# Differential attention: score products alone in one set of PSUM banks, values beside the projections, the output projection cut in steps

## The chip, the core and the metric

The kernel runs on one core of a Trainium2 chip. TensorE (PE) multiplies matrices from SBUF into PSUM, VectorE (DVE) and ScalarE (ACT) do element-wise work and reductions, and queues of transfers (DMA) bring weights from HBM. PSUM has eight banks of 128 x 512 f32; one accumulating product holds one bank. The metric is the time of one execution in microseconds (us), lower is better.

## What is computed

Two networks, one behind the other, on 256 tokens of width 1024. The first has four layers: Fourier mixing, differential attention, latent attention, Fourier mixing, each followed by an MLP of width 4096; the first three layers carry 256 context tokens as well, so their products have 512 columns. The second has two layers of a state-space mixer beside a windowed attention. The change is in layer 1 of the first network, differential attention:

```
def diff_attend(q1, q2, k1, k2, v, lam):
    s1 = einsum("bqhd,bkhd->bhqk", q1, k1) * 64 ** -0.5
    s2 = einsum("bqhd,bkhd->bhqk", q2, k2) * 64 ** -0.5
    p = softmax(s1) - lam * softmax(s2)
    return einsum("bhqk,bkhe->bqhe", p, v)
y = (rms_norm(o, subln_g) * (1 - lam_init)) @ w_o
```

There are eight heads, each with two score matrices and values of width 128. The 256 latent queries see 512 keys, the 256 context queries see the 256 context keys.

## The kernel before

A program written in a tile language: the source gives the work in an order, a scheduler places each instruction on its engine, earlier lines first, later ones ahead of them where the earlier are not ready. A tile is taken from a pool under a tag; `mm` is the tag of four PSUM banks, `aux` that of the other four, `g` that of 41 SBUF tiles.

Products are made in three matmuls of rounded parts (high x high, high x low, low x high; `split` and `loadw` make the parts, a cast on ACT at L396 or L306 and a subtraction on DVE at L397 or L307).

In `diff`, after a start that makes the keys, queries and values of heads 0 and 1, the heads go in four groups of two. A head has three items, `it` 0 and 1 (128 latent queries each, 512 keys) and 2 (the 256 context queries, 256 keys), so a group has six. An item has two steps:

- the scores step, `scores(h, it)`: split the queries (L396, L397), score products into two banks (L1227), row maxima (DVE, L1231, L1233), exponentials (ACT, L1238, into two `g` tiles), their weighted difference (DVE, L1242 to L1247);
- the values step, `values(h, it)`: four transposes of that difference into a bank (L1258), copy to SBUF (ACT, L1260, a `g` tile), four value products, eight matmuls in the trace, into another bank (L1267), copy and squares (ACT, L1269, L1272); after item 2 of a head the root of the mean square and a scaling (DVE, L413 to L421, L1281).

The steps are staggered by one item (`pipe_feed`, lag 1): scores of an item, then "fill" products, then the values step of the item before. Fill of group g is `qkv(g + 1)`: eight tiles, two of keys and two of queries (`kq`, 24 matmuls of 512 columns each, L324 to L327, evacuated by DVE and ACT at L1143 to L1146 and L1183) and four of values (`val`, 24 matmuls of 256 columns, L1199 to L1201, evacuated by ACT at L1202), at 4/3 of a tile to an item. The fill has its banks in `mm`; scores, transposes, values and `finish` have theirs in `aux`.

`finish(h)` transposes a head's output (L1288) and splits it (ACT L1290, DVE L1291, into `g` tiles) for the output projection. It runs in the last group, `DIFF_FIN` says after which items. Fill of the last group is the output projection: `linear_k` holds four output tiles open in all four `mm` banks and adds one head to all four in a step of twelve matmuls (L351 to L353), `DIFF_WO` says how many steps behind which item. The second half of the output projection follows in `tail` (L324 to L327 with 256 columns).

`rows_add(RATES[1])` at each scores step paces unrelated work: units of modulation rows for later layers, each a 1 MB transfer and two or four DVE reductions (L588).

Of the kernel before, what the change touches and what calls it, by code (L numbers as in the profile page):

```python
# [17 lines left out]
P = 128  # L18
# [208 lines left out]
}  # L227
NDT = 5
AHEAD = 200
RATES = (0.35, 0.13, 0.6, 0.0, 0.3)  # L230
START = 12
LEAD = 2
DIFF_WO = (0, 1, 1, 1, 1, 0, 3)
DIFF_FIN = ((0, 1), (2, 3), (4,), (5,), (6,), ())
ORDER = [2, 5, 8, 11, 0, 1, 3, 4, 6, 7, 9, 10] + list(range(12, 24))
SCHED = ((6, 0), (6, 0), (6, 0), (6, 0), (6, 1), (4, 3), (0, 2), (0, 2))
# [5 lines left out]
class Body:  # L242
# [27 lines left out]
    def mm(self, cols=512):  # L270
        return self.ps.tile([P, 512], F32, tag="mm", name=self.nm("mm"))
# [92 lines left out]
    def pipe_feed(self, items, fill, rate):  # L364
        a, b, lag, q = self.pp
        due = 0.0
        for it in items:
            q.append((it, a(*it)))
            due += rate
            while due >= 1.0:  # L370
                next(fill, 0)
                due -= 1.0
            if len(q) > lag:
                it, r = q.pop(0)
                b(*it, r)

    def pipe_end(self, fill, rate):
        a, b, lag, q = self.pp
# [779 lines left out]
    def diff(self, mod, nxt):  # L1158
        nc = self.nc
        I = self.I  # L1160
# [16 lines left out]
        ks, qs, vs = {}, {}, {}  # L1177
# [9 lines left out]
        def kq(g):  # L1187
            yield from self.linear([I["diff_w"][g]], hs, 512, ev_rope(ks), m0=2 * g)
            yield from self.linear([I["diff_w"][8 + g]], hs, 512, ev_rope(qs), m0=2 * g)

        def val(g):
            w = self.loadw(I["diff_w"][4 + g], 8, 256, by="k")
            for j2 in range(2):
                vs[g, j2] = self.g()[:, :512].rearrange("p (j e) -> p j e", e=256)
            for j in range(4):
                ps = self.mm()
                sl = slice(j * P, j * P + P)
                for k in range(8):
                    nc.tensor.matmul(ps[:, :256], hs[k][0][:, sl], w(0, k, 0, 256), start=k == 0, stop=False)  # L1199
                    nc.tensor.matmul(ps[:, :256], hs[k][0][:, sl], w(1, k, 0, 256), start=False, stop=False)  # L1200
                    nc.tensor.matmul(ps[:, :256], hs[k][1][:, sl], w(0, k, 0, 256), start=False, stop=k == 7)  # L1201
                nc.scalar.copy(vs[g, j // 2][:, j % 2, :], ps[:, :256])  # L1202
                yield
# [8 lines left out]
        def scores(h, it):  # L1212


            self.rows_add(RATES[1])
            nq, k0, nk = (1, 0, 512) if it < 2 else (2, 256, 256)
            if h == 0 and it == 0:
                keys(0)
            q = self.split(qs[h][:, it * P:(it + nq) * P])
            if it == 2 and h < 7:  # L1220
                keys(h + 1)
            s = [self.aux(), self.aux()]
            for c in range(nq):
                for n_, (a, b) in enumerate(((0, 0), (0, 1), (1, 0))):
                    for i in range(2):
                        r = slice(64 * i, 64 * i + 64)
                        nc.tensor.matmul(s[i][:, c * nk:c * nk + nk], q[a][r, c * P:c * P + P],  # L1227
                                         kx[h][b][r, k0:k0 + nk], start=n_ == 0, stop=n_ == 2)
            mx, nm, ac, r = [self.sm(4)[:, :2 * nq] for _ in range(4)]
            for i in range(2):  # L1230
                nc.vector.tensor_reduce(out=mx[:, i * nq:i * nq + nq], in_=s[i].rearrange("p (c k) -> p c k", c=nq),  # L1231
                                        axis=AX.X, op=ALU.max)
            nc.vector.tensor_scalar(out=nm, in0=mx, scalar1=-scale, scalar2=None, op0=ALU.mult)  # L1233
            es = [self.g() for _ in range(2)]
            c0 = 4 * h + it
            for i in (1, 0):
                for c in range(nq):
                    nc.scalar.activation(es[i][:, c * nk:c * nk + nk], s[i][:, c * nk:c * nk + nk], AF.Exp,  # L1238
                                         bias=nm[:, i * nq + c:i * nq + c + 1], scale=scale,
                                         accum_out=ac[:, c:c + 1] if i else dac[:, c0 + c:c0 + c + 1])  # L1240

            nc.vector.reciprocal(r[:, :nq], ac[:, :nq])  # L1242
            nc.vector.scalar_tensor_tensor(out=r[:, :nq], in0=r[:, :nq], scalar=nlam, in1=dac[:, c0:c0 + nq],
                                           op0=ALU.mult, op1=ALU.mult)
            for c in range(nq):
                sl = slice(c * nk, c * nk + nk)
                nc.vector.scalar_tensor_tensor(out=es[0][:, sl], in0=es[1][:, sl], scalar=r[:, c:c + 1],  # L1247
                                               in1=es[0][:, sl], op0=ALU.mult, op1=ALU.add)
            return es[0]

        def values(h, it, p):


            g, e0 = h // 2, (h % 2) * P
            nq = 1 if it < 2 else 2
            ps = self.aux()
            for j in range(4):
                nc.tensor.transpose(ps[:, j * P:j * P + P], p[:, j * P:j * P + P], self.ident)  # L1258
            pt = self.g()[:, :512]
            nc.scalar.copy(pt, ps)  # L1260
            if it == 0:
                of[h] = self.g()[:, :512]
            o = self.aux()
            nj = 4 // nq
            for j in range(4):
                jk = j if it < 2 else 2 + j % 2
                nc.tensor.matmul(o[:, j // nj * P:j // nj * P + P], pt[:, j * P:j * P + P],  # L1267
                                 vs[g, jk // 2][:, jk % 2, e0:e0 + P], start=j % nj == 0, stop=j % nj == nj - 1)
            nc.scalar.copy(of[h][:, it * P:(it + nq) * P], o[:, :nq * P])  # L1269
            sq = self.tp.tile([P, 512], F32, tag="sq", name=self.nm("sq"), bufs=2)  # L1270
            for c in range(nq):
                nc.scalar.activation(sq[:, c * P:c * P + P], o[:, c * P:c * P + P], AF.Square,  # L1272
                                     accum_out=dss[:, 4 * h + it + c:4 * h + it + c + 1])
            if it == 2:
                hc = slice(4 * h, 4 * h + 4)
                ep = self.sm(4)
                nc.vector.scalar_tensor_tensor(out=ep, in0=dac[:, hc], scalar=EPS, in1=dac[:, hc],
                                               op0=ALU.mult, op1=ALU.mult)
                self.rstd_of(dss[:, hc], dr[:, hc], 1.0 / P, ep)
                o3 = of[h].rearrange("p (q e) -> p q e", e=P)  # L1280
                nc.vector.tensor_tensor(out=o3, in0=o3, in1=dr[:, hc].unsqueeze(2).to_broadcast([P, 4, P]), op=ALU.mult)  # L1281

        def finish(h):

            ps = self.aux()
            o = of.pop(h)
            for j in range(4):
                nc.tensor.transpose(ps[:, j * P:j * P + P], o[:, j * P:j * P + P], self.ident)  # L1288
            hi, lo = self.pair(512)
            nc.scalar.activation(hi, ps, AF.Copy, scale=sg)  # L1290
            nc.vector.scalar_tensor_tensor(out=lo, in0=ps, scalar=sg, in1=hi.bitcast(F32), op0=ALU.mult,  # L1291
                                           op1=ALU.subtract)
            os_[h] = (hi, lo)

        def ev_kq0(m, ps):
            ev_rope(ks if m < 2 else qs)(m % 2, ps)

        def qkv(g):
            yield from kq(g)
            yield from val(g)  # L1300

        def out(m, ps, streams=BOTH):
            if m == 0:
                self.rows_to(12)
                nxt()
            self.resid(m, ps, streams, mod, 2)
            self.norm_add(m, streams[0][1], streams[-1][2])
# [1 line left out]
        yield from self.head([I["diff_w"][0], I["diff_w"][8]], ev_kq0)  # L1309
        hs = self.nb.hs  # L1310
        yield from val(0)
        wo = self.linear_k([I["diff_w"][12], I["diff_w"][13]], os_, 512, out)
        for g in range(4):
            items = [(h, it) for h in (2 * g, 2 * g + 1) for it in range(3)]
            fill = qkv(g + 1) if g < 3 else wo
            if g == 0:
                self.pipe_begin(scores, values, 1)
            if g < 3:
                self.pipe_feed(items, fill, 4 / 3)
                self.drain(fill)  # L1320
            else:
                for i, it in enumerate(items):
                    self.pipe_feed([it], wo, DIFF_WO[i])
                    for h in DIFF_FIN[i]:
                        finish(h)
            yield
        self.pipe_end(wo, 0)
        for _ in range(DIFF_WO[6]):
            next(wo)
        finish(7)  # L1330
        self.drain(wo)
        yield from self.tail([I["diff_w"][12 + u] for u in (2, 3)], [os_[h] for h in range(8)], out, 4)
# [905 lines left out]
```

## Time and profile before

| | |
|---|---|
| median of 3 runs | 2953.48 us (2946.76 to 2955.89) |
| the profiled execution, its time | 2948.07 us |
| its span | 2946.3 us |
| PE busy | 2863.0 us (97%) |
| DVE busy | 2153.2 us (73%) |
| ACT busy | 1489.9 us (51%) |
| DMA, mean over the span | 156 GB/s |
| mean granted clock of PE | 0.991 |

Busy times are sums over one profiled execution. A line of the trace gives start and duration in us, engine, source line, output and input tiles with their shapes, the count, and in brackets how long the engine had been idle before it and whose end released it. Matmuls overlap in the record, so the distance between starts is a better measure than the duration. PEclk is the granted clock of PE as a share of full speed.

### The profile page before, as it was taken

The numbers are of one execution on the slowest core, as the hardware profiler recorded it, in microseconds if no ns is written. First come the engines' busy times: TensorE is split into PE (matmuls) and PEld (weight loads), VectorE is DVE, ScalarE is ACT, GpSimd is POOL, SyncE is SP. The second block draws the span as 40 slices with busy tenths as digits, with TensorE's granted clock in tenths as the row PEclk, the third lists the DMA queues.
The fourth block names the chain that finished last, engine by engine and source line by source line (L and its number), as shares of the span: only waits on it lengthen the run. The fifth ranks groups of instructions, "written<-read, shape, count | busy, mean of one in ns | idle before, by whom it ended". The sixth has DMA issues, their size and how long they took to land.

```text
span 2946.3 us, 51090 instructions
## 1 busy us (share of the span) xinstructions
PE 2863.0 (97%) x20316; PEld 2593.5 (88%) x20316; DVE 2153.2 (73%) x4707; ACT 1489.9 (51%) x2941; POOL 18.0 (1%) x66
## 2 busy tenths in 40 slices
PE   8999999998999999999999999999999999999999
PEld 6788889886888888599999999988999999989999
DVE  5597667775986667677756789886666799886765
ACT  5433323554432334855555567655554567655553
POOL 1000000000000000000000000000000000000000
PEclk9999999999999999999999999999999999999999
DMA  9454443320375553145525534333444444333553
GB/s 343 172 200 159 170 160 135 115 87 15 129 284 214 205 196 108 43 169 205 199 99 191 184 138 160 132 115 115 146 172 173 146 156 144 129 116 130 185 186 129
DMA packets 70366, 460.81 MB, mean 156 GB/s; under 512 B 7792, under 2 KB 9840, under 8 KB 16752
## 3 DMA queue, kind: packets, MB, share of 16 engines
q1 hardware_dynamic: 69984, 456.51, 43.6%
q8 instruction: 160, 2.62, 0.4%
q10 hardware_dynamic: 144, 1.05, 0.1%
q14 instruction: 78, 0.64, 0.1%
HBM read 456.47 MB, written 1.05 MB: 155 GB/s over the span
## 4 chain that ended last, share of the span: by engine, by line
PE 85%; DVE 8%; ACT 4%; DMA 1%; issue 1%; ACTq 0%; SPq 0%; DVEq 0%
PE mm L324 23%; PE mm L325 23%; PE mm L327 22%; DVE wlo L307 2%; ACT whi L306 1%; PE mm L675 1%; PE mm L674 1%; PE mm L676 1%; PE aux L1267 1%; PE mm L745 1%; PE aux L545 1%; PE mm L746 1%; PE mm L744 1%; DVE t L1701 1%; PE aux L1227 1%
## 5 line engine op out<-in xcount | busy, mean ns | idle before, releaser
L324 PE MATMUL mm<-g,whi 128*128 128x256 f32 (+3 forms) x5008 | 1406.9, 310 | 12.9 <-DVE t L1701 6.0
L325 PE MATMUL mm<-g,whi 128*128 128x256 f32 (+3 forms) x5008 | 1400.4, 308 | 0.5 <-DVE g L397 0.5
L306 ACT CAST whi<-raw 128x1024 fp32r<-128x1024 f32 (+2 forms) x670 | 697.5, 1048 | 821.0 <-PE mm L325 723.7
L324 PEld LDWEIGHTS mm<-g,whi 128*128 128x128 f32 x5008 | 941.6, 188 | 75.6 <-issue 15.7
L325 PEld LDWEIGHTS mm<-g,whi 128*128 128x128 f32 x5008 | 941.3, 188 | 51.7 <-issue 3.1
L307 DVE TENSOR_TENSOR wlo<-raw,whi 128x1024 fp32r<-128x1024 f32 (+2 forms) x670 | 809.5, 1210 | 122.0 <-ACT whi L306 65.7
L327 PE MATMUL mm<-g,wlo 128*128 128x256 f32 (+3 forms) x5008 | 835.2, 308 | 0.0
L327 PEld LDWEIGHTS mm<-g,wlo 128*128 128x128 f32 x5008 | 712.8, 188 | 47.0 <-issue 0.7
L588 DVE CUSTOM_DVE_ANT_0 junk<-raw,silu_b 128x1024 bf16<-128x1024 f32 x208 | 253.8, 1220 | 46.8 <-DMA raw<-in_mod_wT 44.9
L607 DVE SCALAR_TENSOR_TENSOR x<-mm,mod,x 128x256 f32<-128x256 f32 x216 | 98.3, 479 | 129.1 <-PE mm L327 125.4
L769 DVE TENSOR_TENSOR y<-mm,rb 128x256 f32<-128x256 f32 (+1 forms) x144 | 61.3, 427 | 89.8 <-PE mm L327 68.5
L846 DVE TENSOR_TENSOR g<-t,g 128x256 fp32r<-128x256 f32 (+2 forms) x192 | 98.5, 514 | 4.2
L843 ACT ACTIVATE t<-t 128x256 f32<-128x256 f32 (+2 forms) x192 | 94.0, 491 | 8.0 <-DVE g L846 2.9
L1701 DVE SCALAR_TENSOR_TENSOR t<-mm,cwh,t 128x270 f32<-128x270 f32 (+2 forms) x192 | 91.9, 490 | 2.7 <-ACT t L1698 2.4
L2195 DVE TENSOR_TENSOR x<-x,mm 128x272 f32<-128x272 f32 (+1 forms) x64 | 27.5, 429 | 81.0 <-PE mm L327 81.0
L675 PE MATMUL mm<-g,whi 128*128 128x256 f32 x240 | 66.7, 287 | 1.7 <-DVE g L643 1.6
L676 PE MATMUL mm<-g,wlo 128*128 128x256 f32 x240 | 65.5, 282 | 0.0
L841 ACT ACTIVATE t<-mm 128x512 f32<-128x512 f32 x64 | 37.9, 600 | 53.7 <-PE mm L327 53.6
L845 DVE CAST g<-t 128x256 fp32r<-128x256 f32 (+2 forms) x192 | 64.0, 334 | 1.3 <-ACT t L843 0.9
L674 PE MATMUL mm<-g,whi 128*128 128x256 f32 x240 | 60.7, 285 | 2.6 <-ACT g L642 2.6
L744 PE MATMUL mm<-g,whi 128*128 128x258 f32 (+2 forms) x192 | 54.5, 287 | 1.0 <-ACT g L716 0.7
L745 PE MATMUL mm<-g,whi 128*128 128x258 f32 (+2 forms) x192 | 54.7, 286 | 0.3 <-DVE g L717 0.3
(409 smaller groups left out, 3270.9 us busy)
## 6 DMA issues: line engine op xcount, KB each, us to landing
raw<-in_mlp_w SPq DMA_DIRECT2D x128, 1024.0 KB, 4.9
raw<-in_w_in SPq DMA_DIRECT2D x76, 1024.0 KB, 4.9
raw<-in_mod_wT SPq DMA_DIRECT2D x72, 1024.0 KB, 4.9
raw<-in_w_up SPq DMA_DIRECT2D x32, 1024.0 KB, 4.8
raw<-in_w_dn SPq DMA_DIRECT2D x32, 1024.0 KB, 4.8
raw<-in_diff_w SPq DMA_DIRECT2D x16, 1024.0 KB, 4.8
raw<-in_w_sd SPq DMA_DIRECT2D x16, 1024.0 KB, 4.8
raw<-in_mod_w SPq DMA_DIRECT2D x13, 1024.0 KB, 5.3
```

Of the source, the lines that this page charges most:

```text
L306: nc.scalar.copy(hi, v)
L307: nc.vector.tensor_tensor(out=lo, in0=v, in1=hi.bitcast(F32), op=ALU.subtract)
L324: mm(ps, w(0, k, c0, c1), xs[k][0], start=first and k == 0, stop=False)
L325: mm(ps, w(0, k, c0, c1), xs[k][1], start=False, stop=False)
L327: mm(ps, w(1, k, c0, c1), xs[k][0], start=False, stop=last and k == n - 1)
L588: nc.vector.tensor_tensor_reduce(out=self.junk, in0=r[:, D * j:D * j + D], in1=self.silu_b[:, D * s:D * s + D], scale=1.0, scalar=0.0, op0 ...
L607: self.nc.vector.scalar_tensor_tensor(out=self.x[m][:, c0:c1], in0=ps[:, c0:c1], scalar=mod[:, gc * 8 + m, s:s + 1], in1=self.x[m][:, c0:c ...
L675: mm(pss[i][:, c0:c1], w(0, k, o, o + P), l, start=False, stop=False)
L676: mm(pss[i][:, c0:c1], w(1, k, o, o + P), h, start=False, stop=k == 7)
L843: nc.scalar.activation(s[:, :n], t[:, :n], AF.Square)
L846: nc.vector.tensor_tensor(out=lo, in0=s[:, :n], in1=hi.bitcast(F32), op=ALU.subtract)
L1701: nc.vector.scalar_tensor_tensor(out=t[:, sft:L2], in0=ps[:, :L2 - sft], scalar=cw[:, 3 - sft:4 - sft], in1=t[:, sft:L2], op0=ALU.mult, op ...
```

## The change

- `RATES[1]` goes from 0.13 to 0: no modulation rows are issued from the scores steps of this layer.
- The values step takes its two banks from `mm` instead of `aux`, and so does `finish`, except for the last item (7, 2) and for head 7. `aux` is then left to the score products.
- `linear_k` is replaced for this projection by `wo_gen`, in ten steps: seven that add one of heads 0 to 6 to two output tiles (six matmuls each), two that take heads 0 to 6 into one further tile each (21 matmuls), one that adds head 7 to all four (12 matmuls) and evacuates them.
- `held` traces a fill step so that its PE instructions come behind a given matmul in PE's queue: the last score matmul traced, or, after item (7, 2), its last value matmul.
- `val(3)`, the values of the last two heads, goes from the fill of group 2 to the last group, four steps behind the scores of item (6, 0). Group 2 keeps `kq(3)` at 2/3 of a tile to an item.
- `DIFF_WO` then says, for the six items of the last group: 4 (of `val(3)`), 1, 1, 2, 1, 2 steps; one more before the last values step and one behind it.

```
@@ -227,10 +227,10 @@
 }
 NDT = 5
 AHEAD = 200
-RATES = (0.35, 0.13, 0.6, 0.0, 0.3)
+RATES = (0.35, 0.0, 0.6, 0.0, 0.3)
 START = 12
 LEAD = 2
-DIFF_WO = (0, 1, 1, 1, 1, 0, 3)
+DIFF_WO = (4, 1, 1, 2, 1, 2, 1, 1)
 DIFF_FIN = ((0, 1), (2, 3), (4,), (5,), (6,), ())
 ORDER = [2, 5, 8, 11, 0, 1, 3, 4, 6, 7, 9, 10] + list(range(12, 24))
 SCHED = ((6, 0), (6, 0), (6, 0), (6, 0), (6, 1), (4, 3), (0, 2), (0, 2))
@@ -373,6 +373,14 @@
             if len(q) > lag:
                 it, r = q.pop(0)
                 b(*it, r)
+
+    def held(self, gen):
+
+        while True:
+            with self.tc.issue_after(self.behind.ins):
+                if next(gen, self) is self:
+                    return
+            yield
 
     def pipe_end(self, fill, rate):
         a, b, lag, q = self.pp
@@ -1224,8 +1232,9 @@
                 for n_, (a, b) in enumerate(((0, 0), (0, 1), (1, 0))):
                     for i in range(2):
                         r = slice(64 * i, 64 * i + 64)
-                        nc.tensor.matmul(s[i][:, c * nk:c * nk + nk], q[a][r, c * P:c * P + P],
-                                         kx[h][b][r, k0:k0 + nk], start=n_ == 0, stop=n_ == 2)
+                        self.behind = nc.tensor.matmul(
+                            s[i][:, c * nk:c * nk + nk], q[a][r, c * P:c * P + P], kx[h][b][r, k0:k0 + nk],
+                            start=n_ == 0, stop=n_ == 2)
             mx, nm, ac, r = [self.sm(4)[:, :2 * nq] for _ in range(4)]
             for i in range(2):
                 nc.vector.tensor_reduce(out=mx[:, i * nq:i * nq + nq], in_=s[i].rearrange("p (c k) -> p c k", c=nq),
@@ -1253,19 +1262,24 @@
 
             g, e0 = h // 2, (h % 2) * P
             nq = 1 if it < 2 else 2
-            ps = self.aux()
+
+            bank = self.aux if (h, it) == (7, 2) else self.mm
+            ps = bank()
             for j in range(4):
                 nc.tensor.transpose(ps[:, j * P:j * P + P], p[:, j * P:j * P + P], self.ident)
             pt = self.g()[:, :512]
             nc.scalar.copy(pt, ps)
             if it == 0:
                 of[h] = self.g()[:, :512]
-            o = self.aux()
+            o = bank()
             nj = 4 // nq
             for j in range(4):
                 jk = j if it < 2 else 2 + j % 2
-                nc.tensor.matmul(o[:, j // nj * P:j // nj * P + P], pt[:, j * P:j * P + P],
-                                 vs[g, jk // 2][:, jk % 2, e0:e0 + P], start=j % nj == 0, stop=j % nj == nj - 1)
+                last = nc.tensor.matmul(o[:, j // nj * P:j // nj * P + P], pt[:, j * P:j * P + P],
+                                        vs[g, jk // 2][:, jk % 2, e0:e0 + P], start=j % nj == 0,
+                                        stop=j % nj == nj - 1)
+            if (h, it) == (7, 2):
+                self.behind = last
             nc.scalar.copy(of[h][:, it * P:(it + nq) * P], o[:, :nq * P])
             sq = self.tp.tile([P, 512], F32, tag="sq", name=self.nm("sq"), bufs=2)
             for c in range(nq):
@@ -1282,7 +1296,7 @@
 
         def finish(h):
 
-            ps = self.aux()
+            ps = self.aux() if h == 7 else self.mm()
             o = of.pop(h)
             for j in range(4):
                 nc.tensor.transpose(ps[:, j * P:j * P + P], o[:, j * P:j * P + P], self.ident)
@@ -1292,6 +1306,33 @@
                                            op1=ALU.subtract)
             os_[h] = (hi, lo)
 
+        def wo_gen():
+
+
+            mm = nc.tensor.matmul
+            ws = [self.loadw(I["diff_w"][12 + u], 8, 256) for u in range(2)]
+            pss = {}
+
+            def part(m, ks):
+                if m not in pss:
+                    pss[m] = self.mm()
+                w, c0 = ws[m // 2], m % 2 * P
+                for k in ks:
+                    for a, b in ((0, 0), (0, 1), (1, 0)):
+                        mm(pss[m], w(a, k, c0, c0 + P), os_[k][b], start=k == 0 and a + b == 0, stop=k == 7 and a == 1)
+
+            for k in range(7):
+                part(0, (k,))
+                part(1, (k,))
+                yield
+            for m in (2, 3):
+                part(m, range(7))
+                yield
+            for m in range(4):
+                part(m, (7,))
+                out(m, pss[m])
+            yield
+
         def ev_kq0(m, ps):
             ev_rope(ks if m < 2 else qs)(m % 2, ps)
 
@@ -1309,24 +1350,27 @@
         yield from self.head([I["diff_w"][0], I["diff_w"][8]], ev_kq0)
         hs = self.nb.hs
         yield from val(0)
-        wo = self.linear_k([I["diff_w"][12], I["diff_w"][13]], os_, 512, out)
+        wo = wo_gen()
         for g in range(4):
             items = [(h, it) for h in (2 * g, 2 * g + 1) for it in range(3)]
-            fill = qkv(g + 1) if g < 3 else wo
+            fill = kq(3) if g == 2 else qkv(g + 1) if g < 2 else val(3)
             if g == 0:
                 self.pipe_begin(scores, values, 1)
             if g < 3:
-                self.pipe_feed(items, fill, 4 / 3)
+                self.pipe_feed(items, fill, 4 / 3 if g < 2 else 2 / 3)
                 self.drain(fill)
             else:
                 for i, it in enumerate(items):
-                    self.pipe_feed([it], wo, DIFF_WO[i])
+                    self.pipe_feed([it], self.held(wo if i else fill), DIFF_WO[i])
                     for h in DIFF_FIN[i]:
                         finish(h)
             yield
+        held = self.held(wo)
+        for _ in range(DIFF_WO[6]):
+            next(held)
         self.pipe_end(wo, 0)
-        for _ in range(DIFF_WO[6]):
-            next(wo)
+        for _ in range(DIFF_WO[7]):
+            next(held)
         finish(7)
         self.drain(wo)
         yield from self.tail([I["diff_w"][12 + u] for u in (2, 3)], [os_[h] for h in range(8)], out, 4)
```

## Rows read from the trace of the kernel before

**Rows 1.** Windows: stretch, length, busy us of PE, PEld, DVE, ACT, POOL, PEclk, DMA.

```profile
533.60:633.40 99.80, 98.88 (x626) 82.73 (x625) 76.81 (x202) 54.04 (x157) 0.00 (x0) 1.00 0.28 98
633.40:680.60 47.20, 46.71 (x302) 39.23 (x301) 33.20 (x97) 26.27 (x82) 0.00 (x0) 1.00 0.17 61
680.60:745.50 64.90, 49.82 (x261) 37.22 (x261) 34.14 (x98) 28.60 (x89) 0.00 (x0) 0.89 0.05 17
```

**Rows 2.** Timeline of PE, scores and values steps around items (7, 0) and (7, 1).

```profile
709.24 1.06 PE L1227 MATMUL aux<-g,g 64*128 64x512 f32 x6
710.22 0.66 PE L1258 MATMUL aux<-k,g 128*128 128x128 f32 x4
...
713.88 1.16 PE L1267 MATMUL aux<-g,g 128*128 128x128 f32 x8 [0.44 <-ACT g L1260]
714.88 0.60 PE L1288 MATMUL aux<-k,g 128*128 128x128 f32 x4
...
717.27 0.98 PE L1227 MATMUL aux<-g,g 64*128 64x512 f32 x6
...
722.57 1.16 PE L1267 MATMUL aux<-g,g 128*128 128x128 f32 x8 [1.43 <-ACT g L1260]
```

**Rows 3.** Timeline of ACT in the same stretch.

```profile
711.90 0.69 ACT L1238 ACTIVATE g<-aux,sm 128x512 f32<-128x512 f32 x1 [2.96 <-DVE sm L1233]
...
713.25 0.58 ACT L1260 COPY g<-aux 128x512 f32<-128x512 f32 x1
...
716.43 0.32 ACT L396 CAST g<-g 128x128 fp32r<-128x128 f32 x1
```

**Rows 4.** Timeline of PE behind the scores of item (6, 0).

```profile
681.53 0.66 PE L1258 MATMUL aux<-k,g 128*128 128x128 f32 x4
686.68 2.08 PE L1267 MATMUL aux<-g,g 128*128 128x128 f32 x8 [4.49 <-ACT g L1260]
688.54 1.91 PE L1288 MATMUL aux<-k,g 128*128 128x128 f32 x8
```

**Rows 5.** Timeline of PE behind item (7, 2), last values to second half.

```profile
733.51 1.16 PE L1267 MATMUL aux<-g,g 128*128 128x128 f32 x8 [0.67 <-ACT g L1260]
738.64 1.09 PE L1288 MATMUL aux<-k,g 128*128 128x128 f32 x4 [3.97 <-DVE g L1281]
740.51 2.08 PE L351 MATMUL mm<-g,whi 128*128 128x512 f32 x4 [0.78 <-ACT g L1290]
...
745.54 0.28 PE L324 MATMUL mm<-g,whi 128*128 128x256 f32 x1
```

**Rows 6.** Timeline of PE: a tile of keys, a tile of values.

```profile
534.52 0.50 PE L324 MATMUL mm<-g,whi 128*128 128x512 f32 x1
...
540.18 0.40 PE L324 MATMUL mm<-g,whi 128*128 128x512 f32 x1
...
562.89 0.28 PE L1199 MATMUL mm<-whi,g 128*128 128x256 f32 x1
...
565.72 0.60 PE L1258 MATMUL aux<-k,g 128*128 128x128 f32 x4
```

**Rows 7.** Timeline of PE behind a tile of keys, transposes of (1, 2).

```profile
588.46 0.60 PE L1258 MATMUL aux<-k,g 128*128 128x128 f32 x4
588.81 0.47 PE L324 MATMUL mm<-g,whi 128*128 128x512 f32 x1
```

**Rows 8.** Timeline of ACT in the same stretch.

```profile
589.56 0.37 ACT L1183 COPY g<-mm 128x256 f32<-128x256 f32 x1 [0.37 <-DVE t L1144]
589.83 0.59 ACT L1260 COPY g<-aux 128x512 f32<-128x512 f32 x1
```

**Rows 9.** Timeline of PE, windowed attention of the second network.

```profile
2004.69 0.65 PE L2001 MATMUL mm<-ptm,vz 128*64 128x256 f32 x2 [0.20 <-DVE ptm L1992]
```

**Rows 10.** Groups by line from 533.6 to 745.5, modulation rows on DVE.

```profile
L588 DVE CUSTOM_DVE_ANT_0 junk<-raw,silu_b 128x1024 bf16<-128x1024 f32 x8 | 9.7, 1218 | 1.6 <-DMA raw<-in_mod_wT 1.6
```

**Rows 11.** Windows, MLP of layer 1, columns as in rows 1.

```profile
800.00:820.00 20.00, 20.00 (x88) 16.25 (x87) 19.97 (x37) 9.68 (x15) 0.00 (x0) 1.00 0.71 259
```

## Prediction, before the change was run

> **What bounds the kernel now.** The page comes first: PE is busy for 97% of the span, so only stretches in which PE waits can give anything. The windows by stage show where layer 1's attention has them: from the first scores step to the start of group 2 PE idles 99.80 - 98.88 = 0.92 us, in group 2 0.49 us, in group 3 up to the second half of the output projection 64.90 - 49.82 = 15.08 us, with the granted clock at 0.89 [rows 1]. PE's timeline names the waits: 4.49 us behind the scores of (6, 0), 3.97 us ahead of the last `finish`, and 0.4 to 1.5 us ahead of the value products of each item [rows 2, 4, 5]. The two long ones halve the clock behind them: eight value matmuls take 2.08 us against 1.16, eight `finish` transposes 1.91 against some 0.95 (two of the fours that take 0.60 each, overlapping), and the last twelve matmuls of the open tiles 745.54 - 740.51 = 5.03 us against 12/24 of 5.66 = 2.83 [rows 2, 4 to 6]. With the last `finish` (1.09 against 0.60) the slow clock costs 0.9 + 1.0 + 0.5 + 2.2 = 4.6 us. All that the change can win in this layer is 15.08 + 0.92 + 0.49 + 4.6 = 21.1 us.
>
> **What sets these waits.** The reader is to follow item (7, 0). Its scores start at 709.24, the transposes of (6, 2) end at 710.9, ACT is idle for 2.96 us until 711.90, and yet the copy of those transposes starts only at 713.25, behind the exponentials of (7, 0) [rows 2, 3]. Both write `g` tiles, the exponentials first in the source. The queries of (7, 1) are cast at 716.43, behind that copy and behind a `finish`, though they had been there for long [rows 3]. The same in PSUM: for 4.49 us PE did nothing although the transposes of heads 0 and 1 were ready and one of the four `aux` banks was free; they came right behind the value products, whose tile stands ahead of theirs in the source [rows 4]. I read this as: tiles of one tag get their buffers in source order, whether buffers are free or not. Then the loop of an item is closed through `g`: scores, maxima, exponentials, copy of the transposes, value products, `finish`, cast of the next queries, scores. From scores to value products it takes 4.64 and 5.30 us, mean 4.97 [rows 2]; without the scores (0.98) and the transposes (0.35, [rows 7]) PE has 3.6 us to fill. From the end of the value products to the next scores it takes 717.27 - 714.88 = 2.39 us, without `finish` (0.35) 2.0 us. Before, fill tiles in `mm` have nothing to do with `aux` and run in all these holes.
>
> **Scores alone in `aux`: worth nothing.** The next scores wait for the cast of their queries, which stands behind the copy in `g`, not for a bank. The Trainium skill (Perfetto Trace Analysis, Identifying Performance Opportunities) says that the same gap coming again and again on the engine that should be full can mean that there isn't enough SBUF or PSUM for the next tile. By it the four banks would take the waits away; that is the first rival below, and the free bank of [rows 4] speaks against it.
>
> **Values beside the fill in `mm`: the cost.** Now the tile of the next fill stands behind the two tiles of a values step in the same tag. Between the transposes of an item and its value products PE can open nothing. Before it does just that: at 588.81 it starts the next tile [rows 7]. The windowed attention of the second network has this order already (its output and the fill in `mm`), and waits for the copy with fill to spare [rows 9]. The price per values step of groups 0 to 2 is:
>
> - Behind a tile of keys or queries. The tile (5.66 us, [rows 6]) covers the 3.6 us; then come the transposes, to 588.81, and the copy can start only when ACT has evacuated the tile: 589.83, plus 0.59 = 590.42 [rows 7, 8]. Wait 1.6 us.
> - Behind a tile of values (2.83 us, [rows 6]): 3.6 - 2.83 = 0.8 us.
> - Behind both: only transposes, copy, values, 0.67 us as at 733.51 [rows 5].
> - Behind no tile: 3.6 us.
>
> Groups 0 and 1 at 4/3 give 1, 1, 1, 2, 1, 1 tiles and one at the end; the eleven values steps stand behind keys or queries 5 times, behind both 2 times, behind values 4 times: 5 x 1.6 + 2 x 0.67 + 4 x 0.8 = 12.5 us, before 0.92: +11.6. Group 2 at 2/3 gives 0, 1, 0, 1, 1, 0 (the sum of the thirds stays a rounding under 1) and one at the end: 3 x 1.6 + 3 x 3.6 = 15.6, before 0.49: +15.1. Bounds: if the copy came ahead of the tile's evacuation, the 1.6 would be 0.67 (8 x 0.93 = 7.4 us less); if next fill opened all the same, nothing is added (second rival).
>
> **Group 3, with `val(3)`, `wo_gen` and `held`.** PE's work is the same matmuls. `val(3)` fills the 4.49 us behind (6, 0) and the 21 matmuls of the second single-tile step, held behind the last value product (21/24 x 5.66 = 4.95 us) fill the 3.97 us ahead of the last `finish`, so the clock does not fall there: these gains are real. But the loop of the five items between does not get shorter, and it is filled with less: a step is now 6/24 x 5.66 = 1.4 us instead of 2.8, and being held behind the scores it no longer runs ahead of them. From scores to values: three items with one step wait 3.6 - 1.4 = 2.2, two with two steps 0.8: 8.2 us. From values to the next scores 5 x 2.0 = 10.0 us, with no open work allowed in. At the ends: copy behind `val(3)` 0.67, copy behind the first 21 matmuls 0.67, `finish` to head 7's matmuls 0.78 [rows 5]: 2.1 us. Together 20.3 us against 15.08 + 4.6 = 19.7 before: +0.6.
>
> **The clock.** PE waits of 3.97 and 4.49 us were followed by a halved clock, those of 0.4 to 1.5 us were not [rows 2, 4, 5]. The three of 3.6 us in group 2 lie nearest to 3.97; I charge each 0.9 + 1.0 = 1.9 us, 5.6 in all (bounds 0, and 9.4 more if the five of 2.0 to 2.2 us do the same).
>
> **Modulation rows.** `RATES[1] = 0` takes a few units out of this layer; eight reductions of 1.218 us are seen in it [rows 10]. DVE is not what PE waits for here, so it gives nothing. They are done in the MLP behind, where the paced count stays and three more units have four reductions instead of two: 6 x 1.22 = 7.3 us of DVE. DVE is full there in places (19.97 of 20.00 us) while PE waits for nothing (20.00 of 20.00) [rows 11]; PE's own matmuls hide it. I take 0, the bound is +7.3. No DMA is late: the three 1 MB transfers only move.
>
> **Sum.** 11.6 + 15.1 + 0.6 + 5.6 = 32.9 us, on the profiled execution's 2948.07 (span 2946.3 and 1.8 around it): 2981.0 us. Its time is 5.4 us under the median of the three runs, inside their scatter of 9; I leave the sum on it.
>
> **The rivals.**
>
> - *The banks were the limit* (faster, 2930 us). If the next scores do run ahead into the wait for the copy, PE has the next item's work in each hole, and what is left is the 2.1 us at the ends: 2948.1 - 21.1 + 2.1 = 2929 to 2930. For it: four banks for two items' scores, and all 15 us of waits stand ahead of tiles in `aux`. Against it: the cast at 716.43 behind the copy [rows 3], and the free bank [rows 4]. It decides where the new waits of the stage stay under 19 us in sum.
> - *The order in `mm` doesn't bind* (no change, 2949 us). Fill opens across a values step as before; groups 0 to 2 keep their 1.4 us, group 3 gives +0.6. For it: nothing shows the order in `mm` in this layer before. Against it: [rows 4, 9].
> - *More of the same* (slower, 2990 to 2998 us): the waits of 2 us halve the clock too (+9.4), or the moved rows make the MLP's weights late (+7.3). For it: DVE's 19.97 of 20. Against it: 1.43 us waits at full clock.
>
> **Numbers.** Chances: the forecast 0.63, more of the same 0.10, no change 0.11, faster 0.16. The forecast's own range is 2968 (copy ahead of the evacuation, no slow clock: 32.9 - 7.4 - 5.6 = 19.9) to 2998. The range for all reaches down to 2940, past the case of no change, and up to 2998; it leaves out most of the faster case. This kernel can be told from no change by 0.3%, about 9 us; the cases give faster 0.16, same 0.11, slower 0.73.
>
> **What would show it.** Right: in the trace after, PE idle ahead of L1267 in nearly every item of groups 0 to 2 with ACT's copy as releaser, some 28 us up to the scores of (6, 0), three of over 3 us in group 2 with a slow stretch behind; the scores of an item still behind the value products of the item before the last; no wait of 4 us in group 3, but 2 us ahead of L1227 in each item. Wrong: scores of two items back to back on PE, or keys and queries tiles that start between L1258 and L1267.

## The result, and the profile after

The changed kernel takes 2991.31 us (median of 4 runs, 2990.74 to 2998.08), the kernel before 2951.49 us (4 runs): a ratio of 1.0138, interval 1.0122 to 1.0153. The forecast was 2981.0, in a range of 2940 to 2998, slower at 0.73. The profiled execution is the longest of the four (span 2996.3 us, 50.0 over that of before), so the stretches below are compared with each other, not with the medians. Of the 50.0 us, 45.9 lie in the stage that the change touches; what lies behind it takes 5.5 us more, what lies ahead of it 1.4 less.

The windows by stage of the changed kernel, from the first scores to the scores of (4, 0), to those of (6, 0), and to the second half of the projection; they answer to [rows 1]:

```profile
core 0: us, PE busy (x) PEld busy (x) DVE busy (x) ACT busy (x) POOL busy (x), PEclk, DMA share, GB/s
532.20:647.50 115.30, 101.64 (x613) 84.13 (x612) 68.22 (x184) 54.09 (x158) 0.00 (x0) 0.97 0.16 55
647.50:712.12 64.62, 45.51 (x217) 35.09 (x216) 33.79 (x96) 25.92 (x78) 0.00 (x0) 0.87 0.15 49
712.12:789.96 77.84, 64.55 (x357) 51.24 (x357) 34.79 (x99) 29.57 (x88) 0.00 (x0) 0.89 0.04 14
```

The reader is to see length less PE busy: PE idles 13.66, 19.11 and 13.29 us, 46.06 in all, where it idled 0.92, 0.49 and 15.08 before. The stage is 257.76 us long, 45.86 more than before; idle time is 29.6 of that. Most of the rest is the clock (0.97, 0.87 and 0.89 granted). These are the stretches at half clock in the stage:

```profile
core 0: us, PE busy (x) PEld busy (x) DVE busy (x) ACT busy (x) POOL busy (x), PEclk, DMA share, GB/s
584.07:587.49 3.42, 3.42 (x18) 3.42 (x17) 0.00 (x0) 1.55 (x4) 0.00 (x0) 0.50 0.00 0
642.10:645.51 3.41, 3.41 (x16) 3.41 (x17) 0.48 (x2) 0.59 (x4) 0.00 (x0) 0.50 0.00 0
652.34:659.17 6.83, 6.08 (x20) 4.63 (x21) 3.97 (x17) 2.10 (x10) 0.00 (x0) 0.50 0.06 24
...
sum 40.96, PE 38.59 PEld 31.85 DVE 13.76 ACT 14.02 POOL 0.00; mean PE 4.29 PEld 3.54 DVE 1.53 ACT 1.56 POOL 0.00
```

PE works 38.6 us at half speed. At full speed this would take about half as long (eight value products take 1.16 us in place of 2.08), so I put the cost at 19.3 us, an estimate that e10 tests below: 3.4 in groups 0 and 1, 7.6 in group 2, 8.3 in group 3. The two stretches of before (683.79 to 690.62, 738.41 to 745.23) cost 4.9 by the same reading.

PE's waits in the stage, by what ended them (L1278 are the value products, L1271 the copy of the transposes, L1235 the scores, L404 and L405 the split of the queries):

```profile
engine line waited for: us in total, times, longest us
PE mm L1278 <- ACT g L1271: 37.6, 22, 4.1
PE aux L1235 <- ACT g L404: 4.0, 4, 1.5
PE aux L1235 <- DVE g L405: 1.2, 3, 0.6
```

Before, value products waited 9.7 us in 8 places. PE's timeline at three places (L1269 transposes; in brackets the idle time ahead of an instruction and what ended it):

```profile
545.41 0.60 PE L1269 MATMUL mm<-k,g 128*128 128x128 f32 x4
547.40 1.16 PE L1278 MATMUL mm<-g,g 128*128 128x128 f32 x8 [1.39 <-ACT g L1271]
548.32 0.48 PE L324 MATMUL mm<-g,whi 128*128 128x512 f32 x1
...
648.39 0.66 PE L1269 MATMUL mm<-k,g 128*128 128x128 f32 x4
653.09 2.08 PE L1278 MATMUL mm<-g,g 128*128 128x128 f32 x8 [4.04 <-ACT g L1271]
655.10 1.65 PE L1235 MATMUL aux<-g,g 64*128 64x512 f32 x6
...
732.36 0.73 PE L1235 MATMUL aux<-g,g 64*128 64x512 f32 x4 [1.46 <-ACT g L404]
```

At 545.41 transposes, 1.39 us of nothing, values, and only then the next keys tile (L324), where before that tile started behind the transposes [rows 7]. At 648.39 the same with no fill ahead of it: 4.04 us, and the values behind it take 2.08 us in place of 1.16. At 732.36 scores that wait for the cast of their queries, though all of `aux` is theirs.

### The profile page after: what moved, and what is told of

Same layout as the page of the kernel before. It is cut to its first block, busy times and chain, and to the rows that moved or that the text cites. A ratio compares the mean times of both kernels' runs of the same rounds, so it can differ in the third digit from the quotient of the medians.

```text
span 2996.3 us, 51094 instructions
## 1 busy us (share of the span) xinstructions
PE 2883.2 (96%) x20316; PEld 2607.2 (87%) x20316; DVE 2154.9 (72%) x4707; ACT 1490.8 (50%) x2941; POOL 18.0 (1%) x66
## 4 chain that ended last, share of the span: by engine, by line
PE 83%; DVE 9%; ACT 5%; DMA 1%; issue 1%; ACTq 0%; DVEq 0%; SPq 0%
PE mm L324 23%; PE mm L325 22%; PE mm L327 22%; DVE wlo L307 3%; PE mm L1278 1%; PE mm L683 1%; ACT whi L306 1%; PE mm L682 1%; PE mm L684 1%; ACT g L1247 1%; PE aux L1235 1%; PE mm L753 1%; PE mm L754 1%; PE mm L752 1%; DMA raw<-in_mlp_w 1%
## 5 line engine op out<-in xcount | busy, mean ns | idle before, releaser
L324 PE MATMUL mm<-g,whi 128*128 128x256 f32 (+3 forms) x5008 | 1411.2, 311 | 14.7 <-DVE t L1745 6.0
L324 PEld LDWEIGHTS mm<-g,whi 128*128 128x128 f32 x5008 | 945.5, 189 | 80.0 <-issue 16.3
L683 PE MATMUL mm<-g,whi 128*128 128x256 f32 x240 | 66.7, 286 | 1.7 <-DVE g L651 1.6
L1278 PE MATMUL mm<-g,g 128*128 128x128 f32 x184 | 30.5, 316 | 37.6 <-ACT g L1271 37.6
L1247 ACT ACTIVATE g<-aux,sm 128x512 f32<-128x512 f32 (+1 forms) x64 | 36.5, 578 | 57.9 <-DVE sm L1242 47.2
L1278 PEld LDWEIGHTS mm<-g,g 128*128 128x128 f32 x184 | 25.8, 216 | 43.6 <-ACT g L1271 43.5
```

The lines of the kernel that those rows point to most:

```text
L324: mm(ps, w(0, k, c0, c1), xs[k][0], start=first and k == 0, stop=False)
L683: mm(pss[i][:, c0:c1], w(0, k, o, o + P), l, start=False, stop=False)
```

## The experiments

Eleven kernels. Idle time and slow clock were read for each as above, in one profiled execution of each kernel, between the same four points. The stage is the whole from the first scores to the second half of the projection, "slow clock" the estimated cost of the stretches at half clock, in us by the same groups; "-" is under 0.1. Code is shown in short.

| kernel | median, us | ratio to before, 95% | stage, us | PE idle, groups 0-1 / 2 / 3 | slow clock |
|---|---|---|---|---|---|
| before | 2950.1 to 2951.5 | | 211.9 | 0.9 / 0.5 / 15.1 | - / - / 4.9 |
| changed | 2991.3 | 1.0122 to 1.0153 | 257.8 | 13.7 / 19.1 / 13.3 | 3.4 / 7.6 / 8.3 |
| e1 values in `aux` | 2955.5 | 1.0004 to 1.0029 | 217.0 | 0.9 / 3.6 / 14.5 | - / 0.5 / 6.1 |
| e2 output bank early | 2963.1 | 1.0030 to 1.0068 | 220.7 | 1.0 / 5.5 / 12.8 | - / 1.7 / 6.6 |
| e3 before, values in `mm` | 2974.2 | 1.0056 to 1.0103 | 234.7 | 13.5 / 7.5 / 13.5 | 1.7 / - / 4.9 |
| e4 before, rate 0 | 2953.2 | 0.9992 to 1.0014 | 212.9 | 0.9 / 0.6 / 15.1 | - / - / 5.2 |
| e5 fill back | 2984.5 | 1.0100 to 1.0130 | 238.7 | 13.6 / 7.5 / 17.2 | - / - / 6.1 |
| e10 pads | 2987.3 | 1.0108 to 1.0153 | 248.5 | 1.8 / 4.3 / 13.6 | - / - / 6.7 |
| e6 queries' own tile | 2950.5 | 0.9989 to 1.0010 | 207.1 | 4.8 / 5.3 / 4.4 | - / - / - |
| e9 the same, pairs of banks | 2954.7 | 1.0008 to 1.0032 | 202.6 | 0.3 / - / 6.2 | - / - / 1.7 |
| e7 before, queries' own tile | 2947.3 | 0.9974 to 0.9994 | 205.0 | 1.3 / 0.7 / 9.9 | - / - / 4.5 |
| e11 before, own tile and pairs | 2943.5 | 0.9963 to 0.9985 | 201.6 | 0.8 / 0.2 / 3.9 | - / - / 3.3 |
| e12 changed, own tile and pairs | 2944.1 | 0.9970 to 0.9989 | 204.1 | 0.3 / - / 6.2 | - / - / 3.4 |

**Is it the place of the values?** One part undone (e1), one part alone (e3):

```
e1: - bank = self.aux if (h, it) == (7, 2) else self.mm
    + bank = self.aux if h < 6 or (h, it) == (7, 2) else self.mm
e3 (in before): + bank = self.mm if h < 6 else self.aux     # for ps and o in values
```

> The changed kernel with the values step of heads 0 to 5 back in aux; group 3 and the fill of 2/3 in group 2 as changed. Theory (the values tiles in mm bar the next fill tile): PE's idle time in groups 0 and 1 falls from 13.7 us to about 1 and their 3.4 us of slow clock go; in group 2 the holes can be filled again, but with two thirds of a tile to an item the loop of an item, some 7.4 us, sets the pace: idle from 19.1 to about 8, slow clock from 7.6 to about 2. Sum 12.7 + 3.4 + 11 + 5.6 = 33 us less: about 2958 us. Rival (the thin fill of group 2 and the smaller steps of group 3 are the cost, not the place of the values): groups 0 and 1 gain their 16 us and group 2 nothing: 2975 us.

> The kernel before with one part alone: the values step of heads 0 to 5 in mm. Theory (order in mm): groups 0 and 1 get the 12.7 us of idle time and 3.4 us of slow clock that the changed kernel shows, group 2, still filled at 4/3, half of that again: 2951 + 24 = 2975 us. Rival (the loss comes from the thin fill and the cut projection, and order in mm does not matter): 2951 us.

e1, its windows by stage:

```profile
533.05:631.19 98.14, 97.24 (x614) 81.18 (x613) 66.75 (x183) 52.79 (x156) 0.00 (x0) 1.00 0.19 65
631.19:672.86 41.67, 38.07 (x217) 29.29 (x217) 33.45 (x98) 24.85 (x78) 0.00 (x0) 0.99 0.23 77
672.86:750.03 77.17, 62.68 (x357) 50.64 (x357) 33.62 (x97) 30.22 (x91) 0.00 (x0) 0.92 0.04 14
```

Of the 45.9 us that the stage lost, 257.8 - 217.0 = 40.8 go with the place of the values, the other 5.1 with the thin fill, the cut projection and the rate together; no run tells these three apart in this kernel. Group 2 kept 3.6 us of idle time, not the 8 expected: with `mm` free, two thirds of a tile nearly suffice. e3 shows the same from the other side, 2974.2 against 2975 expected.

**Order or number of banks?** e2 leaves the values in `mm` and the order of the tiles, and only opens the output's bank before the wait:

```
  for j in range(4): nc.tensor.transpose(ps[:, ...], p[:, ...], self.ident)
+ o = bank()
+ if h < 6: nc.tensor.transpose(o[:, :P], p[:, :P], self.ident)   # overwritten by the values
  pt = self.g()[:, :512]; nc.scalar.copy(pt, ps)
```

> The changed kernel, values of heads 0 to 5 still in mm, but each output bank is opened ahead of the copy: one more transpose (128 columns, its result overwritten by the value products) is written into it right behind the transposes. Number of banks and order of tiles stay. Theory (the fill tile waits because the output tile ahead of it in the source has not been opened yet): fill starts in the wait again, and the gain is that of the values in aux, 33 us, less 18 transposes of some 0.1 us: about 2960 us. Rival (four mm banks are too few for values and fill): no gain, 2991 to 2993 us.

PE's timeline of e2 at the place shown above (L1272 is the extra transpose, L1280 the values):

```profile
546.91 0.60 PE L1269 MATMUL mm<-k,g 128*128 128x128 f32 x4
547.35 0.27 PE L1272 MATMUL mm<-k,g 128*128 128x128 f32 x1
547.37 0.48 PE L324 MATMUL mm<-g,whi 128*128 128x512 f32 x1
...
549.56 1.05 PE L1280 MATMUL mm<-g,g 128*128 128x128 f32 x8
```

The next keys tile starts 0.02 us after the extra transpose does, and the 1.39 us are gone: 2963.1 us, 28 less than the changed kernel, with no bank added and 18 instructions more. The wait was one of order. The Trainium skill (Perfetto Trace Analysis, Identifying Performance Opportunities) says that a gap which repeats on the engine that should be full can mean too little SBUF or PSUM for the next tile. Here the gap did come back with every item, and what waited was the next tile in PSUM, but the number of banks was enough: the 1.39 us went with the same four, one of them taken earlier.

**Does the cost depend on the fill ahead of the wait?** e5 makes `val(3)` in group 2 again, at 4/3:

```
- fill = kq(3) if g == 2 else qkv(g + 1) if g < 2 else val(3)
+ fill = qkv(g + 1) if g < 3 else iter(())          # rate 4/3 in all three, DIFF_WO[0] = 0
```

> The changed kernel with one part undone: the values of heads 6 and 7 are made in group 2 again, whose fill is 4/3 of a tile to an item as before; values in mm, cut projection and held steps stay. Theory (a values step in mm waits the shorter, the more fill lies ahead of it): group 2 pays what half of groups 0 and 1 pay, 6.8 us of idle time and 1.7 of slow clock in place of 19.1 and 7.6, 18 us less; the wait behind the scores of (6, 0) comes back with its slow clock, some 6 us: about 2979 us. Rival (a values step in mm costs the same whatever the fill): only the 6 us, 2997 us.

Group 2 of e5:

```profile
644.25:701.82 57.57, 50.09 (x314) 41.31 (x313) 35.20 (x99) 27.77 (x82) 0.00 (x0) 1.00 0.16 56
```

It does: group 2 idles 7.5 in place of 19.1 us, and its clock stays full. Group 3 took the wait of [rows 4] back (4.04 us) and idles 17.2. The stage is 19.1 us shorter than in the changed kernel, the median only 6.8: 2984.5 lies 5.5 over the theory's 2979 and 12.5 under the rival's 2997. In the profile, 6.2 us of the gain are lost again behind the stage, where the instructions are the same; the last section comes back to this.

**What is the clock worth by itself?** e10 keeps the waits of groups 0 to 2 and puts matmuls of no use into them:

```
+ PADS = ((5, 5, 3), (3, 7, 5), (5, 5, 3), (3, 7, 16), (5, 16, 5), (5, 16, 5))
  (in values, behind the transposes, h < 6:)
+ with self.tc.issue_after(tlast.ins):
+     for _ in range(PADS[h][it]):
+         nc.tensor.matmul(pad, kp[:, :P], kp[:, :512], start=True, stop=True)
```

> The changed kernel with idle time of PE filled by matmuls of no use: behind the transposes of each values step of heads 0 to 5, 3 to 16 extra matmuls (512 columns, 0.23 us each at full clock) into a bank of aux that nobody reads, about as many as fit the wait seen there. The waits for the copy stay as long, PE is only not idle in them. Theory (half of what the prediction missed is the clock that falls behind waits of 1.8 to 4.1 us): the half-speed stretches of groups 0 to 2 go and with them 3.4 + 7.6 us: about 2980 us. Rival (the slow clock costs nothing by itself, since the matmuls in it would have waited anyway): 2991 us, or some 2 more for matmuls that do not fit the wait.

Its timeline at the place of the 4.04 us (L1275 pads, L1284 values) and its windows of groups 0 to 2:

```profile
645.84 0.66 PE L1270 MATMUL mm<-k,g 128*128 128x128 f32 x4
646.25 3.90 PE L1275 MATMUL aux<-g 128*128 128x512 f32 x16
650.53 1.16 PE L1284 MATMUL mm<-g,g 128*128 128x128 f32 x8 [0.37 <-ACT g L1277]
```

```profile
532.81:644.95 112.14, 110.32 (x665) 89.43 (x665) 68.24 (x184) 54.01 (x158) 0.00 (x0) 1.00 0.17 57
644.95:702.70 57.75, 53.47 (x282) 41.05 (x281) 33.67 (x96) 25.91 (x78) 0.00 (x0) 1.00 0.15 55
```

The wait for the copy is as long (from the start of the transposes to the values 4.69 us, in the changed kernel 4.70), the values take 1.16 us again, and the two stretches are 3.2 and 6.9 us shorter than in the changed kernel, close to the 3.4 and 7.6 read as the price of the clock. In the medians the 11 us expected are only 4, and the intervals of the two ratios overlap: the stretches show the price, the whole time doesn't.

**What holds the scores back?** e6 gives the split of the queries an SBUF tile of its own (and `g` 40 tiles in place of 41); e7 does it in the kernel before:

```
- q = self.split(qs[h][:, it * P:(it + nq) * P])
+ qt = self.mixp.tile([P, 512], F32R, tag="q", bufs=1); q = qt[:, :n], qt[:, n:2 * n]   # n = nq * P
+ nc.scalar.copy(q[0], src); nc.vector.tensor_tensor(out=q[1], in0=src, in1=q[0].bitcast(F32), op=ALU.subtract)
```

> The changed kernel with the split of an item's queries in an SBUF tile of its own, not among the g tiles (whose number is 40 in place of 41). Theory (the next scores stand behind the copy of the transposes by the order of g, not for want of a bank): scores go into the wait for the copy; each of the 18 waits of groups 0 to 2 gets about 1 us shorter, the long ones of group 2 by more, the waits ahead of the scores in group 3 go, and with them a good part of the 19 us of slow clock: some 35 us less, about 2956 us. Rival (four aux banks or the exponentials hold the scores back, not g): 2991 us.

> The kernel before with the queries' own tile alone; values stay with the scores in aux. Theory (two orders hold the scores back, that of g and that of aux): the next scores can start right behind the value products, but not ahead of them, since their banks stand behind the output's. The 2 us between values and scores in group 3 go, the waits ahead of the values stay: idle there from 15.1 to about 9, 2951 - 6 = 2945 us. Rival (g alone holds them back): scores go into the waits as well, idle in group 3 about 5, 2938 us.

PE's timeline of e6 (L1274 transposes, L1240 scores of the next item, L1283 values):

```profile
547.62 0.60 PE L1274 MATMUL mm<-k,g 128*128 128x128 f32 x4
548.15 0.99 PE L1240 MATMUL aux<-g,q 64*128 64x256 f32 x12
550.08 1.16 PE L1283 MATMUL mm<-g,g 128*128 128x128 f32 x8 [0.94 <-ACT g L1276]
```

In e6 the scores go into the wait, and the change loses its 41 us: 2950.5. In e7 group 3's idle time falls to 9.9, where 9 were expected of two orders and 5 of one; the median is 2947.3, where 2945 and 2938 were expected. PE's timeline of e7 behind the scores of (6, 0) (L1263 transposes, L1272 values, L1293 `finish`, L1232 scores):

```profile
682.42 0.66 PE L1263 MATMUL aux<-k,g 128*128 128x128 f32 x4
686.10 1.16 PE L1272 MATMUL aux<-g,g 128*128 128x128 f32 x8 [3.02 <-ACT g L1265]
687.09 1.73 PE L1293 MATMUL aux<-k,g 128*128 128x128 f32 x8
688.75 1.65 PE L1232 MATMUL aux<-g,q 64*128 64x512 f32 x6
```

With values and scores in one tag the scores can follow the values without a wait but not pass them. Banks of their own let the scores run ahead only once their queries no longer stand in `g`.

**Three orders apart.** e9 (from the changed kernel) and e11, e12 (from before, from the changed kernel) add to the queries' tile a pair of banks for scores and a pair for values and `finish`, so that fill is alone in `mm`:

```
+ tag = "aux" if scores else "auv"     # 2 banks each; elsewhere the two take turns
+ s = [self.aux("aux"), self.aux("aux")];  ps, o = self.aux("auv"), self.aux("auv")
```

> The changed kernel with the queries' own tile as in the run above, and the four aux banks as two pairs with a name each: one for scores, the other for values and finish, so that fill is alone in mm. Theory (three orders that do not hold each other up: scores, values, fill): PE idles about 0 in groups 0 and 1, some 2 us in group 2, some 5 in group 3, and the slow clock costs 2 to 4 us: 2991 - 46 - 19 + 10 = about 2936 to 2942 us, below the kernel before. Rival (the loop of an item is bound by VectorE and ScalarE, and PE waits for them however the tiles are named): about the 2955 us of the run with the values in aux.

> The kernel before with the queries' own tile and the two pairs of banks, scores alone in one, values and finish in the other, fill alone in mm; the pairs hold for the first network only, the second has its four aux banks under one name again. Group 2 is filled at 4/3 and the projection is taken in steps of twelve as before. Theory (the attention gains, and the 13 us lost behind it in the run with pairs everywhere were lost in the second network): group 3 from 15 us of idle time and 5 of slow clock to about 6 and 2, groups 0 to 2 at 0: 2951 - 13 = about 2938 us. Rival (the loss came with the 40 g tiles or with the pairs in the first network): 2950 us.

> The changed kernel with the queries' own tile and the pairs of banks in the first network only. Theory: the attention takes 9 us less than before, as in the run with pairs everywhere, and the second network as much as before: 2951 - 9 = about 2942 us. Rival (the loss came with the 40 g tiles or with the pairs in the first network): 2954 us.

e9 was expected at 2936 to 2942 and took 2954.7: the stage did shrink, to 202.6 us, but from the second half of the projection to the end it takes 2950.6 - 734.13 = 2216.5 us. e12 is the same with one name for the four banks in the second network, and takes 2944.7 - 740.40 = 2204.3 there. Before, it is 2946.3 - 745.54 = 2200.8. So most of the miss was the two names taken in turns elsewhere: 12.2 of the 15.7 us lost there come from the second network alone (PE idles 52.3 us in that stretch of e9, 46.4 in e12, and is busy 6.3 us longer), and the medians of the two differ by 10.6. Windows by stage and PE's timeline of e11 (L1268 transposes, L1237 scores, L329 fill, L1277 values):

```profile
532.70:631.57 98.87, 98.06 (x614) 82.14 (x614) 75.93 (x202) 54.29 (x158) 0.00 (x0) 1.00 0.27 95
631.57:680.98 49.41, 49.25 (x313) 41.21 (x313) 35.35 (x99) 27.94 (x82) 0.00 (x0) 1.00 0.19 65
680.98:734.31 53.33, 49.43 (x261) 38.39 (x261) 32.06 (x99) 28.59 (x86) 0.00 (x0) 0.94 0.06 21
```

```profile
545.90 0.60 PE L1268 MATMUL auv<-k,g 128*128 128x128 f32 x4
546.43 0.99 PE L1237 MATMUL aux<-g,q 64*128 64x256 f32 x12
547.35 0.51 PE L329 MATMUL mm<-g,whi 128*128 128x512 f32 x1
...
548.61 1.05 PE L1277 MATMUL auv<-g,g 128*128 128x128 f32 x8
```

Transposes, scores of the next item, fill, values, with no idle time: e11 takes 2943.5 us, 0.26% under before (0.15 to 0.37), e12 2944.1. The gains are smaller than expected, 6.7 us for 13 and 6.1 for 9, though e11's stage is 10.3 us shorter than before. Both beat the two kernels given; against each other they can't be told apart, so the moved `val(3)` and the cut projection give nothing that these runs can tell, once the orders are apart.

**The modulation rows** (e4: `RATES = (0.35, 0.0, ...)` alone in before):

> The kernel before with RATES[1] = 0 alone. Theory (VectorE is not what PE waits for, and PE's matmuls hide the moved units in the MLP): no change, 2951 us within 3. Rival (three units more in the MLP make its weights late by their 6 x 1.22 us): 2958 us.

2953.2 us, ratio 0.9992 to 1.0014: no change, as forecast.

## Why the prediction was right, and where its sum was off

The direction, the place and the mechanism of the idle time held; what a wait does to the clock did not. Against the sum:

| term | forecast, us | measured, us |
|---|---|---|
| idle, groups 0 and 1 | 12.5 | 13.7 |
| idle, group 2 | 15.6 | 19.1 |
| idle, group 3 | 20.3 | 13.3 |
| slow clock | 5.6 | 19.3 |
| together | 54.0 | 65.4 |
| the same before | 21.1 | 21.4 |

- **Order in `mm`**: right, and shown by e2. The price by kind of fill held for most steps: in groups 0 and 1 1.36 to 1.39 us behind a tile of keys or queries (1.6 forecast), 0.73 behind both (0.67), 0.79 and 0.82 behind two of the four tiles of values (0.8). The other two waited 1.83 and 1.86 us: there the scores come in the middle of the tile (at 577.31 and 636.43), and only 2.0 us of it are left to fill the wait. In group 2 the three steps behind a tile waited 1.36, 1.36 and 1.64 us, the three without fill 4.04 to 4.11, not 3.6: the 3.6 was a mean over items with fill, taken from group 3. Another 2.5 us of group 2 lie ahead of scores (0.54, 0.48 and 1.51); the sum had nothing for them.
- **Scores alone in `aux` are worth nothing**: right as the kernel stands; e6 shows that `g` was the reason, and what it is worth without it.
- **Group 3**: the gain of `val(3)` behind (6, 0) is there, no wait ahead of L1278 is over 2.5 us. The 10.0 us put ahead of the scores were too many: 4.2 (1.51 + 0.61 at (6, 0) and 1.46 + 0.38 and 0.23 behind), of which the 1.51 count in group 2. So the forecast sign of 2 us ahead of the scores of each item did not come: the transposes of the item before and `finish` stand in that hole and fill most of it. That the group came out near, 21.6 us of idle time and slow clock for 20.3, is luck: the idle time was 7.0 too high, and the 8.3 of slow clock were put at nothing.
- **The clock** is the term that was mis-sized: 19.3 against 5.6. The step said that waits of 0.4 to 1.5 us leave the clock full and charged the three long ones alone. The long ones cost 7.6 for 5.6. But two waits of 1.83 and 1.86 us in groups 0 and 1 were followed by half clock as well (3.4), and so were waits of 1.46 to 2.50 us in group 3 (8.3). The third rival, more of the same, had this as its first half: its 9.4 us for five waits of 2 us in group 3 were near to the 8.3 measured there. The measured time lies in that rival's 2990 to 2998, and in the forecast's own range because the upper bound of that range took the rival in.
- **Idle time in sum** (48.4 forecast, 46.1 measured) came out by errors that cancel in part: group 3 was 7.0 too high, the rest 4.7 too low.
- **Modulation rows**: no cost, as said; e4 shows it by itself.

The time came out 10 us over the forecast. In the profiled execution the stage is 45.9 us longer for 32.9 forecast: 44.0 of it are idle time and clock. Of the 11.1 us that these two were missed by, the clock alone would make 13.7; 2.3 us too much idle time and 0.3 too little cost before take the rest back.

## What to carry to other kernels

Where a scheduler hands out the buffers of a tag in source order, a tile that can only be opened late holds up every tile behind it in that tag, however many buffers are free; look in the trace for an engine that idles between two steps of one item and starts unrelated work right behind the second. Before giving an operation more banks, ask which order its operands stand in: here four free banks did nothing until the queries' split left `g`. And price a wait of PE with the clock behind it: here 46 us of idle time cost some 19 more.

## What the runs showed of the hardware

The same wait can cost the clock or not. In e3 two value steps of the same kind follow waits of 1.82 and 1.84 us:

```profile
585.54 1.80 PE L1268 MATMUL mm<-g,g 128*128 128x128 f32 x8 [1.82 <-ACT g L1261]
...
644.91 1.16 PE L1268 MATMUL mm<-g,g 128*128 128x128 f32 x8 [1.84 <-ACT g L1261]
```

The first stands at the start of a stretch at half clock (585.88 to 589.29), the second at full clock. In the changed kernel both waits of this kind in groups 0 and 1 were followed by half clock, in e5, with the same instructions there, neither of them (1.83 and 1.84 us). The two kernels idle 13.7 and 13.6 us in these groups and take 115.3 and 112.2: 3.1 us for the same work, near to the 3.4 that the slow clock of the one was put at. What decides between them these runs don't show. The three waits of 4.04 to 4.11 us in group 2 of the changed kernel were all followed by half clock; it had fallen by the end of each.

Half clock also moves the rest of the program about. Behind the stage the profiles of e1 and e5 record the same matmuls, and PE idles 47.1 and 46.4 us, but it is busy 13.0 us longer in e5:

```profile
750.03:2950.30 2200.27, 2153.21 (x16141) 2008.02 (x16139) 1648.36 (x3568) 1176.74 (x2288) 10.27 (x38) 1.00 0.45 159
770.76:2983.30 2212.54, 2166.19 (x16141) 2017.64 (x16139) 1649.22 (x3568) 1177.42 (x2288) 10.04 (x38) 0.99 0.45 158
```

By the estimate above, the stretches at half clock there cost 6.5 us in e1 and 18.7 in e5, and 13.1 in the changed kernel; over all thirteen profiles it is 6.4 to 19.2. So what a stage gains need not be seen in full in one time of the whole.
